# A transformer step on one core: x loaded straight to its place, g applied inside the splits, and a new order at the start

## The chip, the cores and the metric

The kernel runs on one core of one Trainium2 chip. The core has a matrix engine (TensorE, PE in the profile, with PEld for its weight loads), a vector engine (VectorE, DVE), a scalar engine (ScalarE, ACT), a general engine (GpSimd, POOL) and a queue engine (SyncE, SP) that here only issues transfers. Each works through its own queue in order; they wait for each other by semaphores. The metric is the device time of one execution in microseconds, and the profile shows one such execution.

## The reference

One layer of a streaming encoder, for a prompt of 1024 tokens and a sample of 64 tokens, 1088 in all, each of width 1024, in float32:

```
xn = rms_norm(x, g_attn)             # x * rsqrt(mean(x*x)) * g
[rq|rk|rv|rg|sq|sk|sv|ga|gb] = split(xn @ w_in)
a = rms_norm(retention(rope(rq), rope(rk), rv)) * silu(rg) @ w_ret_out
b = window_attention(sq, sk, sv) @ w_swa_out
x += (sigmoid(ga) * a + sigmoid(gb) * b) @ w_mix_out
x += cross_attention(rms_norm(x, g_cross), memory)
x += swiglu(rms_norm(x, g_ffn));  y = rms_norm(x, g_final)
```

The factor rsqrt(mean(x*x)) of a token is a scalar of its column, so the kernel multiplies the raw projections by it afterwards. The vector g runs along the contracted dimension and has to be applied to x (or to the weights) before the product.

## The kernel before

The tokens are the columns: x is held transposed, as 8 tiles of 128 features by 1088 tokens (xT in DRAM). A float32 product is made of three fast ones: each operand is split in a high half, rounded to the format the fast product reads, and a low half, the rest. `split` (L122) does it with a cast on ACT (L123) and a subtraction on DVE (L124). A matrix product is a sum of wh·xh, wh·xl and wl·xh (L205, L206, L208).

The large projections take a pair of weight tiles at a time, in seven half-size products instead of eight (Strassen's scheme, in Winograd's form; `strassen`, L247). It needs x in four quarters, B11, B12 (features 0 to 511, tokens 0 to 543 and 544 to 1087), B21, B22 (features 512 to 1023), and four sums of them: T1 = B12 - B11, T2 = B22 - T1, T3 = B22 - B12, T4 = B21 - T2. Each of these eight operands has 4 tiles of 128x544, split in two halves. The order in which a weight pair uses them is B11, B21, T2, T1, T3, B22, T4 (weights P1, P2, P6, P5, P7, P3, P4; `weight_ops`, L166, forms those with GpSimd, ACT and DVE).

The first pair (the first values, w_v) is computed by `plain` (L225), in eight products from the quarters alone: B11 twice and B12, then B21 twice and B22, then B12 and B22. So it can start while the sums are being formed. `start_phase` (L408), the function that changes, prepares it:

- x comes in 16 pieces of 128x544 into four staging buffers xr, and ACT multiplies each by g into its place xg (L430). A load waits until the multiply has emptied its buffer.
- Behind the pieces of B11 and of B12 a half of the raw weights is loaded (`columns`).
- `operands_early` (L1295) splits B11 and B12, `plain_weights` (L217) the four weight tiles, `operands_late` (L1310) B21 and B22, then forms and splits T1 (through `first_sums`, L1305), T2, T3, T4, each in place of a quarter.

The same `operands_early`, `first_sums` and `operands_late` serve the feed-forward part later, where the tiles come out of a computation and not from DRAM.

After the first pair come, for head 0, the keys (w_k) and queries (w_q) by Strassen's scheme, each rotated on DVE and GpSimd (`rotated`, L581) and stored to DRAM; meanwhile `token_squares` (L443) loads x again and adds up its squares on ACT and DVE into rstd (L452, L454), `token_roots` (L456) turns them into the factors of the tokens (a product with the ones, L463), and `retention` (L691) reads the rotated rows back and transposes them on TensorE (L688).

The program text is not the order on the engines. A planner simulates the kernel and sets each engine's queue, preferring what stands first in the text among what it holds ready. `issue_after(ins)` ties the instructions of a block behind `ins` on its engine; `high_priority` puts a block first.

Of the kernel before, what the change touches and what calls it, by code (L numbers as in the profile page):

```python
# [11 lines left out]
F32 = mybir.dt.float32  # L12
F32R = mybir.dt.float32r
AF = mybir.ActivationFunctionType
ALU = mybir.AluOpType
# [4 lines left out]
P = 128  # L20
D = 1024
KT = D // P
# [17 lines left out]

HALF = T // 2
HC = HALF // 2
OPS = ("B11", "T1", "T2", "B21", "T3", "B22", "T4", "B12")


# [64 lines left out]
class Kernel:  # L110
# [86 lines left out]
    def multiply(self, ps, w, xs, first=True, last=True):  # L197

        mm = self.nc.tensor.matmul
        for k, x in enumerate(xs):  # L200
            ks = slice(k * P, (k + 1) * P)
            start, stop = first and k == 0, last and k == len(xs) - 1
            for c in range(2):
                cs = slice(c * HC, (c + 1) * HC)
                mm(ps[:, c, :HC], w[:, 0, ks], x[:, 0, cs], start=start, stop=False)  # L205
                mm(ps[:, c, :HC], w[:, 0, ks], x[:, 1, cs], start=False, stop=False)  # L206
            for c in range(2):
                self.last_mm = mm(ps[:, c, :HC], w[:, 1, ks], x[:, 0, c * HC:(c + 1) * HC], start=False, stop=stop).ins  # L208
        return ps[:, :, :HC]

# [36 lines left out]
    def strassen(self, w, x, emit, part=False):  # L247


        nc = self.nc  # L250
        u1, u2, u3, u5 = (self.fp.tile([P, 2, HC], F32, tag=t, bufs=1, name=t) for t in ("u1", "u2", "u3", "u5"))
        add = lambda out, a, b: nc.vector.tensor_tensor(out=out, in0=a, in1=b, op=ALU.add)  # L252
# [80 lines left out]
    def run(self):  # L333
        nc, tc, io = self.nc, self.tc, self.io
        with ExitStack() as ctx:
# [25 lines left out]
            self.d_h = [dp.tile([KT, P, T], F32, name=f"d_h{i}") for i in range(2)]  # L361
            self.d_op = dp.tile([len(OPS), FT // 2, P, HALF], F32, name="d_op")
            self.d_rb = dp.tile([16, 64 * 256], F32, name="d_rb")
# [44 lines left out]
    def start_phase(self, ctx):  # L408

        nc, tc, io = self.nc, self.tc, self.io  # L410
        g = self.gains[:, 0, :]
        xg = self.ring_tiles(0, KT // 2, "xg", F32)
        self.xg = [xg[k // 2][:, k % 2, :] for k in range(KT)]
        self.ops, self.slots = {}, {}
        self.new_b12(ctx)
        sp = ctx.enter_context(tc.tile_pool(name="sp", bufs=1, reuse_waits="tile"))
        self.early = [sp.tile([P, 2, HC], F32, name=f"early{i}") for i in range(4)]
        xr = lambda: sp.tile([P, HALF], F32, tag="xr", bufs=4, name="xr")
        raws = [self.wp.tile([P, 1024], F32, tag="raw", bufs=2, name="raw") for i in range(2)]

        def columns(j):
            for i in range(2):
                self.load(raws[i][:, j * 512:(j + 1) * 512].rearrange("p (k m) -> p k m", m=P), io["w_v"][i][:, 4 * j:4 * j + 4])

        def pieces(k0, t):
            hs = slice(t * HALF, (t + 1) * HALF)
            for k in range(k0, k0 + 4):
                x = xr()
                self.load(x, io["xT"][k, :, hs])
                nc.scalar.mul(self.xg[k][:, hs], x, g[:, k:k + 1])  # L430

        for n, (k0, t) in enumerate(((0, 0), (0, 1), (4, 0), (4, 1))):
            pieces(k0, t)
            if n < 2:
                columns(n)
            if n == 1:
                self.operands_early()
        self.load(self.ident, io["c_ident"])
        w = self.plain_weights(raws)
        self.operands_late(self.first_sums)  # L440
        return w

    def token_squares(self):  # L443
# [863 lines left out]
            b11, b12, _, _ = self.quarters(k)  # L1307
            self.put_sum("T1", k, b12, b12, b11)

    def operands_late(self, sums=None):  # L1310
        self.op_tiles(1, ("B21", "B22", "T2", "T3"))
        qs = [self.quarters(k) for k in range(4)]
        for k, (b11, b12, b21, b22) in enumerate(qs):
            self.put_op("B21", k, b21)
        for k, (b11, b12, b21, b22) in enumerate(qs):
            self.put_op("B22", k, b22)
        if sums is not None:
            sums()
        for k, (b11, b12, b21, b22) in enumerate(qs):
            self.put_sum("T2", k, b12, b22, b12)  # L1320
        for k, (b11, b12, b21, b22) in enumerate(qs):
            self.put_sum("T3", k, b11, b12, b11)
        self.op_tiles(0, ("T4",))
        for k, (b11, b12, b21, b22) in enumerate(qs):
            self.put_sum("T4", k, b21, b21, b12)
# [15 lines left out]
    def gate_up(self, pairs):  # L1341
# [12 lines left out]
        for n, fs in enumerate(pairs):  # L1354
# [5 lines left out]
            def save(name, src, n=n):  # L1360
                self.store(self.d_op[OPS.index(name), n], src)

# [67 lines left out]
    def fetch(self, name, group):  # L1430
        n0 = sum(GROUPS[:group]) // 2
        for k in range(GROUPS[group] // 2):
            self.pools = self.pools[1:] + self.pools[:1]
            a = self.pools[0].tile([P, HALF], F32, tag="hl", name="hl")
            self.load(a, self.d_op[OPS.index(name), n0 + k])
            yield a
# [179 lines left out]
```

## Time and profile before

| what | us |
|---|---|
| median of 3 runs | 2260.78 (2258.72 to 2265.74) |
| the profiled execution | 2262.17 |
| its span | 2260.3 |
| mean granted TensorE clock | 0.983 |
| ACT, POOL busy | 896.4, 691.1 |

A row of the timeline gives the start and the duration in microseconds, the engine, the line of the kernel, the operation, its output and inputs with their shapes (partitions x elements) and how many were merged; a bracket gives the idle time of the engine before it and what ended that. A row of waits gives who waited for whom: microseconds in total, times, longest. A group's row gives count, busy time, mean ns of one, then the idle time before them and who ended it. Matmuls overlap, so the distance from start to start tells the pace, not the duration.

### The profile page before, as it was taken

To read this page: it belongs to the slowest core of one execution; us is meant where nothing else is said; L and a number is where in the kernel's file an instruction comes from. 1 tells how busy PE (TensorE), PEld (TensorE's weight loads), DVE (VectorE), ACT (ScalarE), POOL (GpSimd) and SP (SyncE) were. 2 spreads that over 40 slices of the span, in tenths; PEclk is the share of its full clock that TensorE was granted. 3 is DMA by queue.
4 is the path that set the end of the run, shared out by engine and by line. 5 is a ranking of instruction groups with operands and counts; after the bars stand their busy time and mean duration, and the time that the engine had idled before them with its cause. 6 is when DMAs were issued, how large, how long until landed. Compare 5 with 4: busy or idle time off the path is not lost.

```text
span 2260.3 us, 42100 instructions
## 1 busy us (share of the span) xinstructions
PE 2170.2 (96%) x16580; PEld 2117.9 (94%) x16580; DVE 1587.3 (70%) x2673; ACT 896.4 (40%) x1923; POOL 691.1 (31%) x467
## 2 busy tenths in 40 slices
PE   7999999999999989999999999999999999999996
PEld 6999998999999977889999998999999999999996
DVE  8986877766677657885455565776777677778497
ACT  7333333345444355553133343333222222344244
POOL 1441533242244112220000000014556555434462
PEclk9999999999999989999999999999999999999998
DMA  5644445443444466326443112422342332476233
GB/s 191 191 139 133 131 143 143 131 136 113 151 156 148 155 223 203 114 77 214 124 153 118 38 53 69 135 73 88 121 134 94 101 129 80 154 256 195 72 97 108
DMA packets 186408, 298.67 MB, mean 132 GB/s; under 512 B 40514, under 2 KB 111074, under 8 KB 186210
## 3 DMA queue, kind: packets, MB, share of 16 engines
q1 hardware_dynamic: 181602, 287.06, 40.4%
q10 hardware_dynamic: 4608, 8.91, 1.1%
q8 instruction: 131, 2.15, 0.4%
q14 instruction: 67, 0.55, 0.1%
HBM read 204.75 MB, written 91.16 MB: 131 GB/s over the span
## 4 chain that ended last, share of the span: by engine, by line
PE 77%; DVE 12%; DMA 5%; ACT 3%; issue 2%; POOL 1%; SPq 0%; DVEq 0%; ACTq 0%; POOLq 0%
PE pq L205 15%; PE pq L208 15%; PE pq L206 15%; PE pd L149 7%; PE pd L151 7%; PE pd L150 7%; DVE wq L124 2%; DVE B L124 1%; DVE T L124 1%; DMA cs<-c_rope 1%; PE pss L930 1%; DMA hl<-d_op 1%; PE pout L996 1%; PE pp L973 1%; DVE stage L562 1%
## 5 line engine op out<-in xcount | busy, mean ns | idle before, releaser
L123 ACT CAST wq<-raw 128x512 fp32r<-128x512 f32 (+1 forms) x509 | 310.2, 614 | 569.3 <-PE pq L208 289.3
L124 DVE TENSOR_TENSOR wq<-raw,wq 128x512 fp32r<-128x512 f32 (+1 forms) x509 | 450.3, 888 | 120.7 <-ACT wq L123 118.7
L205 PE MATMUL pq<-T,wq 128*128 128x272 f32 x1832 | 503.4, 292 | 4.1 <-DVE T L124 2.7
L206 PE MATMUL pq<-T,wq 128*128 128x272 f32 x1832 | 499.7, 289 | 0.0
L205 PE MATMUL pq<-B,wq 128*128 128x272 f32 x1592 | 439.2, 293 | 11.3 <-ACT wq L123 10.2
L206 PE MATMUL pq<-B,wq 128*128 128x272 f32 x1592 | 437.3, 291 | 9.1 <-DVE B L124 8.9
L208 PE MATMUL pq<-T,wq 128*128 128x272 f32 x1832 | 384.5, 290 | 0.7 <-DVE wq L124 0.6
L183 POOL TENSOR_TENSOR raw<-raw 128x512 f32<-128x512 f32 (+1 forms) x59 | 81.2, 1377 | 890.2 <-DVE wq L124 665.7
L205 PEld LDWEIGHTS pq<-T,wq 128*128 128x128 f32 x1832 | 347.3, 190 | 5.4 <-ACT wq L123 3.6
L206 PEld LDWEIGHTS pq<-T,wq 128*128 128x128 f32 x1832 | 350.6, 191 | 0.3 <-issue 0.3
L208 PE MATMUL pq<-B,wq 128*128 128x272 f32 x1592 | 333.9, 290 | 0.0
L206 PEld LDWEIGHTS pq<-B,wq 128*128 128x128 f32 x1592 | 305.9, 192 | 11.8 <-DVE B L124 11.4
L205 PEld LDWEIGHTS pq<-B,wq 128*128 128x128 f32 x1592 | 303.0, 191 | 12.0 <-ACT wq L123 10.2
L208 PEld LDWEIGHTS pq<-T,wq 128*128 128x128 f32 x1832 | 287.2, 190 | 2.2 <-DVE wq L124 1.5
L208 PEld LDWEIGHTS pq<-B,wq 128*128 128x128 f32 x1592 | 250.1, 190 | 0.5 <-issue 0.3
L252 DVE TENSOR_TENSOR u<-pq,u 128x544 f32<-128x544 f32 x177 | 127.5, 720 | 121.8 <-PE pq L208 121.1
L186 POOL TENSOR_TENSOR raw<-raw 128x512 f32<-128x512 f32 (+1 forms) x59 | 83.2, 1410 | 126.1 <-DVE wq L124 118.4
L562 DVE TENSOR_TENSOR stage<-pq,u 128x544 f32<-128x544 f32 x112 | 80.2, 716 | 28.4 <-PE pq L208 28.3
L958 POOL TENSOR_TENSOR t<-t,den 128x768 f32<-128x768 f32 (+2 forms) x34 | 47.8, 1406 | 145.7 <-DVE den L956 58.4
L184 POOL TENSOR_TENSOR raw<-raw 128x512 f32<-128x512 f32 (+1 forms) x59 | 87.2, 1477 | 3.7
L1450 POOL TENSOR_TENSOR y<-u,y 128x544 f32<-128x544 f32 x38 | 63.3, 1674 | 72.8 <-DVE y L1448 52.9
L189 POOL TENSOR_TENSOR raw<-raw 128x512 f32<-128x512 f32 (+1 forms) x59 | 83.7, 1418 | 4.5
(361 smaller groups left out, 4662.6 us busy)
## 6 DMA issues: line engine op xcount, KB each, us to landing
hl<-d_op SPq DMA_DIRECT2D x85, 272.0 KB, 4.3
d_qkv<-stage SPq DMA_DIRECT2D x44, 272.0 KB, 4.4
d_op<-stage SPq DMA_DIRECT2D x44, 272.0 KB, 2.3
d_op<-ht SPq DMA_DIRECT2D x44, 272.0 KB, 3.5
raw<-w_gate SPq DMA_DIRECT2D x22, 512.0 KB, 3.5
raw<-w_up SPq DMA_DIRECT2D x22, 512.0 KB, 4.3
cs<-c_rope SPq DMA_DIRECT2D x16, 544.0 KB, 4.4
d_gate<-stage ACTq DMA_DIRECT2D x32, 272.0 KB, 2.5
```

The lines of the kernel that those rows point to most:

```text
L123: self.last_cast = self.nc.scalar.copy(hi, src).ins
L124: self.nc.vector.tensor_tensor(out=lo, in0=src, in1=hi.bitcast(F32), op=ALU.subtract)
L149: mm(ps, wh, xh, start=start, stop=False)
L150: mm(ps, wh, xl, start=False, stop=False)
L151: self.last_mm = mm(ps, wl, xh, start=False, stop=stop).ins
L184: tt(out=a21, in0=a21, in1=a22, op=add)
L189: tt(out=a12, in0=a12, in1=a11, op=sub)
L205: mm(ps[:, c, :HC], w[:, 0, ks], x[:, 0, cs], start=start, stop=False)
L206: mm(ps[:, c, :HC], w[:, 0, ks], x[:, 1, cs], start=False, stop=False)
L208: self.last_mm = mm(ps[:, c, :HC], w[:, 1, ks], x[:, 0, c * HC:(c + 1) * HC], start=False, stop=stop).ins
L252: add = lambda out, a, b: nc.vector.tensor_tensor(out=out, in0=a, in1=b, op=ALU.add)
L562: nc.vector.tensor_tensor(out=o, in0=ps, in1=sb, op=ALU.add)
```

## The change

Only `start_phase` changes; `operands_late` loses an argument that nobody else used.

- x is loaded straight into xg, all 16 pieces at once, without staging buffers and without the multiply by g. The weights' halves are loaded in between, by single tile (`columns(i, j)`).
- The split of a quarter applies g itself (`put`): ACT multiplies into the high half, DVE forms x·g minus the high half in one instruction with two operations (scalar_tensor_tensor).
- For the sums, B11 and B12 are multiplied by g in place on ACT, 8 instructions; where T2 is formed from B22 and T4 from B21, the same two-operation instruction applies g.
- The splits come in the order B11, B12, B21, B22, with the four weight splits among those of B11 and B12. All sums are tied behind the last split of B21 on ACT and on DVE. The T's are split in the order T2, T1, T3, T4. T3 is now formed from T2 and B11, the same value.
- Ahead of it all ACT multiplies one column of the ones into a spare tile, which is where its table is loaded, and TensorE makes 20 products of the ones with themselves (WARM = 20) whose result nobody reads.

```diff
+WARM = 20
...
-        xr = lambda: sp.tile([P, HALF], F32, tag="xr", bufs=4, name="xr")
...
+        nc.scalar.mul(self.mtok[:, :1], self.ones[:, :1], 1.0)
+        warm = self.norm_psum("warm")
+        for i in range(WARM):
+            nc.tensor.matmul(warm[:, :P], self.ones, self.ones, start=i == 0, stop=i == WARM - 1)
+
+        def rows(k, t):
             hs = slice(t * HALF, (t + 1) * HALF)
-            for k in range(k0, k0 + 4):
-                x = xr()
-                self.load(x, io["xT"][k, :, hs])
-                nc.scalar.mul(self.xg[k][:, hs], x, g[:, k:k + 1])
-
-        for n, (k0, t) in enumerate(((0, 0), (0, 1), (4, 0), (4, 1))):
-            pieces(k0, t)
-            if n < 2:
-                columns(n)
-            if n == 1:
-                self.operands_early()
+            self.load(self.xg[k][:, hs], io["xT"][k, :, hs])
+
+        def columns(i, j):
+            self.load(raws[i][:, j * 512:(j + 1) * 512].rearrange("p (k m) -> p k m", m=P), io["w_v"][i][:, 4 * j:4 * j + 4])
+
+        rows(0, 0)
+        columns(0, 0)
+        for k in range(1, 4):
+            rows(k, 0)
+        columns(1, 0)
+        for k in range(4):
+            rows(k, 1)
+        for i in range(2):
+            columns(i, 1)
+        for t in range(2):
+            for k in range(4, KT):
+                rows(k, t)
         self.load(self.ident, io["c_ident"])
-        w = self.plain_weights(raws)
-        self.operands_late(self.first_sums)
+
+        self.op_tiles(0, ("B11", "T1"))
+        self.ops["B12"] = [self.b12[:, k] for k in range(4)]
+        self.op_tiles(1, ("B21", "B22", "T2", "T3"))
+        qs = [self.quarters(k) for k in range(4)]
+
+        def put(name, k, src, g):
+            o = self.ops[name][k]
+            hi = nc.scalar.mul(o[:, 0], src, g).ins
+            return hi, nc.vector.scalar_tensor_tensor(o[:, 1], src, g, o[:, 0].bitcast(F32), ALU.mult, ALU.subtract).ins
+
+        w = {}
+
+        def weight(i, j):
+            q = w[i, j] = self.new_op()
+            self.split(raws[i][:, j * 512:(j + 1) * 512], q[:, 0, :512], q[:, 1, :512])
+
+        for n, name in enumerate(("B11", "B12", "B21", "B22")):
+            for k in range(4):
+                put_by = put(name, k, qs[k][n], g[:, k + 4 * (n // 2):k + 4 * (n // 2) + 1])
+                if n == 2:
+                    behind = put_by
+                if k == 0 and n < 2:
+                    weight(0, n)
+                if k == 2 and n < 2:
+                    weight(1, n)
+        with tc.issue_after(behind[0]), tc.issue_after(behind[1]):
+            for k in range(4):
+                b11, b12 = qs[k][:2]
+                for b in (b11, b12):
+                    nc.scalar.mul(b, b, g[:, k:k + 1])
+                nc.vector.tensor_tensor(out=b12, in0=b12, in1=b11, op=ALU.subtract)
+        for k, (b11, b12, b21, b22) in enumerate(qs):
+            nc.vector.scalar_tensor_tensor(b22, b22, g[:, k + 4:k + 5], b12, ALU.mult, ALU.subtract)
+            self.put_op("T2", k, b22)
+        for k, (b11, b12, b21, b22) in enumerate(qs):
+            self.put_op("T1", k, b12)
+        for k, (b11, b12, b21, b22) in enumerate(qs):
+            self.put_sum("T3", k, b11, b22, b11)
+        self.op_tiles(0, ("T4",))
+        for k, (b11, b12, b21, b22) in enumerate(qs):
+            nc.vector.scalar_tensor_tensor(b21, b21, g[:, k + 4:k + 5], b22, ALU.mult, ALU.subtract)
+            self.put_op("T4", k, b21)
         return w
```

More of the change, by code (lines that the diff above doesn't have):

```diff
@@ L417, in start_phase @@
         self.early = [sp.tile([P, 2, HC], F32, name=f"early{i}") for i in range(4)]
-        xr = lambda: sp.tile([P, HALF], F32, tag="xr", bufs=4, name="xr")
         raws = [self.wp.tile([P, 1024], F32, tag="raw", bufs=2, name="raw") for i in range(2)]
[L421 to L425, printed above, removed]
-            hs = slice(t * HALF, (t + 1) * HALF)
-            for k in range(k0, k0 + 4):
-                x = xr()
-                self.load(x, io["xT"][k, :, hs])
-                nc.scalar.mul(self.xg[k][:, hs], x, g[:, k:k + 1])
@@ L1308, in first_sums, with operands_late @@
             self.put_sum("T1", k, b12, b12, b11)
-    def operands_late(self, sums=None):
+    def operands_late(self):
         self.op_tiles(1, ("B21", "B22", "T2", "T3"))
@@ L1316, in operands_late @@
             self.put_op("B22", k, b22)
-        if sums is not None:
-            sums()
         for k, (b11, b12, b21, b22) in enumerate(qs):
```

## The prediction

> **What bounds the kernel now.** I first read the summary's busy shares: TensorE is busy 96% of the span, so the question is where the other 4% lies and which part of it the change can reach. All the edited code sits in the first 50 us. The table by stage (columns: busy time and instructions of PE, its weight loads, DVE, ACT and POOL, then granted clock, DMA share, GB/s) shows these stretches:
>
> ```profile
> PE 2170.2 (96%) x16580; PEld 2117.9 (94%) x16580; DVE 1587.3 (70%) x2673; ACT 896.4 (40%) x1923; POOL 691.1 (31%) x467
> ...
> 0.00:10.00 10.00, 0.00 (x0) 0.00 (x0) 1.99 (x5) 5.96 (x9) 0.20 (x4) 1.00 0.77 244
> 10.00:20.00 10.00, 9.82 (x67) 9.82 (x68) 9.07 (x15) 10.00 (x19) 0.00 (x0) 1.00 0.92 299
> 20.00:30.00 10.00, 6.32 (x47) 5.65 (x45) 10.00 (x13) 10.00 (x18) 3.32 (x2) 1.00 0.39 124
> 30.00:40.00 10.00, 7.98 (x59) 7.54 (x60) 10.00 (x17) 4.87 (x9) 0.00 (x0) 1.00 0.15 57
> 40.00:50.00 10.00, 9.90 (x79) 9.69 (x78) 9.28 (x13) 7.21 (x13) 3.38 (x2) 1.00 0.57 192
> 50.00:60.00 10.00, 10.00 (x82) 10.00 (x82) 8.47 (x14) 5.22 (x9) 1.18 (x1) 1.00 0.88 297
> 80.00:90.00 10.00, 8.06 (x65) 7.96 (x65) 9.44 (x12) 2.48 (x5) 9.21 (x6) 0.92 0.49 156
> 90.00:100.00 10.00, 8.45 (x51) 8.16 (x50) 8.75 (x19) 3.08 (x6) 4.65 (x3) 0.74 0.39 116
> 100.00:120.00 20.00, 16.75 (x120) 16.02 (x119) 16.24 (x38) 5.14 (x10) 7.26 (x5) 0.91 0.47 138
> ```
>
> Two things are to be seen. TensorE does nothing for 10 us, then loses 3.7 + 2.0 us between 20 and 40, is full from 40 to 80, and loses 1.9 + 1.6 + 3.3 us between 80 and 120. DVE, by contrast, has hardly a gap from 10 to 100. So early on there are two clocks: TensorE's, with over 15 us to win, and DVE's, with little. Which one sets the end is the whole question. The waits of TensorE in the first 110 us, and the timeline rows around the gaps (start, duration, engine, line, operation, tiles, and in brackets the idle time before), name the causes:
>
> ```profile
> PE pq L205 <- ACT wq L123: 10.2, 1, 10.2
> PE pq L206 <- DVE B L124: 5.5, 3, 2.6
> ...
> 1.17 2.78 DMA xr<-xT
> ...
> 4.02 1.28 ACT L430 ACT_TABLE_LOAD   x1 [4.02 <-DMA xr<-xT]
> 5.32 1.39 ACT L430 ACTIVATE xg<-xr,gains 128x544 f32<-128x544 f32 x2
> 6.61 0.63 ACT L123 CAST B<-xg 128x544 fp32r<-128x544 f32 x1
> 7.27 0.72 DVE L124 TENSOR_TENSOR B<-xg,B 128x544 fp32r<-128x544 f32 x1 [6.26 <-ACT B L123]
> ...
> 10.58 0.43 PE L206 MATMUL pq<-B,wq 128*128 128x272 f32 x1
> 10.80 0.43 PE L205 MATMUL pq<-B,wq 128*128 128x272 f32 x1
> ...
> 13.70 0.29 PE L205 MATMUL pq<-B,wq 128*128 128x272 f32 x1
> 13.82 0.29 PE L206 MATMUL pq<-B,wq 128*128 128x272 f32 x1
> ...
> 42.80 0.29 PE L205 MATMUL pq<-B,wq 128*128 128x272 f32 x1
> ```
>
> The first product waits 10.2 us for ACT, which is loading a table, multiplying x by g and casting. Its first matmuls start 0.22 us apart, from 13.70 on 0.125 us: the slow clock lasts some 3 us. Three times B21 and B22 come late from DVE (5.5 us in all), because the sums for T1 to T4 stand between them. At 42.80 the first eight-product block (24 us of matmuls) is over and the next weight pair begins.
>
> **The change part by part.** All durations are from this one execution: 2262.17 us, of which the span is 2260.3. The median of the three runs shown is 2260.78, 1.4 us less; I subtract from the median.
>
> *Early table load.* The 1.28 us at 4.02 move before the data, to the time when ACT only waits. ACT's first product of x then starts at 4.0 instead of 5.32: 1.3 us, hidden behind the first transfer. [...]
>
> *g inside the split.* Before, an operand costs ACT a multiply and a cast, and DVE a subtraction. After, ACT multiplies straight into the high half, DVE forms the low half with a scalar_tensor_tensor that multiplies and subtracts. So 16 casts go, and 8 extra multiplies (B11 and B12 for the sums) come on top of the 16. The work per tile in the list by form, and the nearest rows of both DVE operations at one shape:
>
> ```profile
> L430 ACT ACTIVATE xg<-xr,gains 128x544 f32<-128x544 f32 x16 | 11.7, 746 | 0.0
> ...
> L123 ACT CAST B<-xg 128x544 fp32r<-128x544 f32 x24 | 14.9, 641 | 0.6 <-DVE xg L1256 0.3
> ...
> L269 DVE SCALAR_TENSOR_TENSOR xc<-ld,gains,xc x24: 546/618/620, 1145.4 to 1238.1; 128x384 fp32r<-128x384 f32 x16, 128x320 fp32r<-128x320 f32 x8
> ...
> L124 DVE TENSOR_TENSOR mix<-ld,mix x24: 491/558/561, 1055.1 to 1141.5; 128x384 fp32r<-128x384 f32 x16, 128x320 fp32r<-128x320 f32 x8
> ```
>
> ACT: 8 multiplies more (8 x 0.75) less 16 casts (16 x 0.64): 4 us less, on an engine that is full from 10 to 30. DVE: the medians are 618 against 558 ns, 0.06 us more each. The count on DVE stays 52 (16 low halves, 4 weight splits, 16 sums, 16 low halves of T), 24 of them of the dearer kind (16 halves, 4 sums for T2, 4 for T4): 24 x 0.06 = 1.4 us lost. Bounds: 0 if the extra time overlaps the instruction before, 2.4 at 0.1 each.
>
> *x straight to its place.* The same 16 loads of x and 4 of w_v, so nothing on the DMA side but the order; no load waits for one of four staging buffers any more. Their 5.5 MB at the 299 GB/s of the second stretch take 18.4 us, so the last piece lands near 21. B21's last piece has 4.4 MB ahead of it and itself, landing near 17, its halves ready near 18.5; TensorE wants it at about 19. SP's queue gets freer, which helps the w_k loads and the identity behind.
>
> *Products of ones.* 20 matmuls of 128x128 in float32, two instructions each. The nearest rows are a fast-clock and a slow-clock group of that form:
>
> ```profile
> 223.38 1.16 PE L473 MATMUL pb<-ident,rtok 128*128 128x128 f32 x8
> 224.30 0.37 PE L206 MATMUL pq<-T,wq 128*128 128x272 f32 x1
> ...
> 2251.46 1.65 PE L1539 MATMUL pb<-ident,rs_f 128*128 128x128 f32 x6 [1.29 <-DVE rs_f L294]
> ```
>
> Fast: 0.92 us for 4 products, 0.23 each. Slow: (1.65 - 0.42) / 5 x 2 = 0.49 each. The ones are there at 1.0 us; with 3.3 us of slow clock, as from 10.18 on, 7 products are slow and 13 fast: 3.3 + 3.0, so they end at 7.5. The first product of w_v could otherwise begin at 3.95 (x landed) + 0.65 + 0.52 (weight cast) with its load a little later, near 5.7. So the ones cost 1.8 us of start and buy 13 matmul steps of 0.1 us, 1.3 us. Bounds: ending at 6 (fast early) to 10.9 (20 x 0.49, slow throughout).
>
> *Order of use.* With B21 and B22 split ahead of all sums, DVE has 20 operations (20 x 0.64 + 16 x 0.06 = 13.8 us) from 4.65 on, with some 2 us of waiting for data, as now (rows below: 10.87 us busy in the 12.73 from 7.27 on): all B's are ready at 20.4, against 25.6 when TensorE reaches B22. The 5.5 us of stalls go. The new wait (the sums issue behind B21's last split on ACT and on DVE) holds 8 multiplies and 4 subtractions, and behind them the T's. T2 comes at 20.4 + 4 x 0.64 + 8 x 0.67 + three weight halves at 0.6 = 30.1; the third product of w_k wants it at 7.5 + 24.1 + 6.0 = 37.6. Cover: 7 us.
>
> **The sum.** TensorE's clock: start 10.18 to 7.5 is 2.7, slow clock 1.3, stalls 5.5: 9.5 us by the time the next weight pair begins. DVE's clock: it starts 2.6 us earlier (7.27 to 4.65), loses 1.4 to the dearer operation, keeps its early waits, wins the 0.7 of idle between 40 and 50, the 1.1 for which the sum of squares waits for ACT (row below; the squares can start when the first block ends), and some 0.5 between 80 and 90: 3.5 us. What decides is the first point at which TensorE must wait for DVE. The rows for it, from the table by stage, DVE's waits from 50 to 60, and TensorE's timeline:
>
> ```profile
> 7.27:20.00 12.73, 9.82 (x67) 9.82 (x68) 10.87 (x17) 12.73 (x23) 0.00 (x0) 1.00 0.93 303
> ...
> 48.90:97.20 48.30, 44.72 (x337) 44.11 (x335) 46.21 (x61) 20.85 (x36) 24.13 (x14) 0.93 0.62 193
> ...
> DVE rstd L454 <- ACT xsq L452: 1.1, 1, 1.1
> ...
> 85.34 2.05 PE L463 MATMUL pt<-ones,rstd 128*128 128x2 f32 x18
> 89.33 1.12 PE L688 MATMUL pk<-ident,ks 128*128 128x128 f32 x4 [1.94 <-DMA ks<-d_qkv]
> 90.70 0.43 PE L205 MATMUL pq<-B,wq 128*128 128x272 f32 x1
> ```
>
> Between 48.9 and 97.2 DVE is busy 46.2 of 48.3 us. The transposes of the first retention block wait for rows which DVE has rotated and which went out and back through DRAM; the sums of squares (L454) are DVE's too. An earlier TensorE only waits longer there. I expect 3.5 to 4 us of the 9.5 to reach the end: 2260.8 - 3.8 = 2257. After 120 us TensorE is nearly full and carries the shift on. Own range of this case: 2254 to 2259, from the bounds on the dearer operation and about 1 us either way for DVE's waits for data.
>
> **Rivals.** (a) *TensorE's clock carries*: what DVE still owes at 85 can be put off, or the products of the next pair are set ahead of the transposes. For it: TensorE did run a w_k product at 90.70 between two transposes. Against it: the row of 46.2 in 48.3. It gives 2260.8 - 9.5 = 2251.
>
> (b) *A wait replaces the removed one*: the first w_k halves stand on DVE behind all sums, which are now always ready. DVE ends its 52 operations at 4.65 + 1.9 + 52 x 0.64 + 1.4 = 41.2, so the next pair begins near 41 instead of 42.8, and 0 to 2 us are left: 2260.
>
> (c) *Slower*: the order on each engine is planned for the whole program, so a start that moves 10 us is a new order everywhere behind. Its place would be the retention's output transposes, which already wait:
>
> ```profile
> L812 PE MATMUL pb<-ident,ret_o 128*128 128x128 f32 x64 | 13.2, 296 | 11.7 <-ACT ret_o L808 11.7
> ```
>
> Waits of over 2 us are followed by the slow clock (0.226 us steps from 90.70 on, clock 0.74), worth 0.1 us x 26 matmuls. If these 11.7 us double, and two of the waits bring the slow clock, 11.7 + 5 - 3.8 = 13 us are lost: 2274. From 3.8 us of new waits on it is a loss. I take a half as typical, 2268. For it speaks only that the waits exist.
>
> (d) *The ones overrun*: should the clock stay slow through all 20, they end at 10.9, TensorE starts 0.7 later than now, and its clock still wins 1.3 + 5.5 - 0.7 = 6.1, over DVE's 3.5; the end would lose at most 1 us: 2258. [...]
>
> **How the numbers follow.** Chances: forecast 0.45, (a) 0.25, (b) 0.12, (c) 0.13, (d) 0.05. A measurement of this kernel can tell about 0.3%, 6.8 us, from no change; so 2254 and 2267.6 are the limits. Faster: nearly all of (a), 0.23, and the lower edge of the forecast, 0.11. Slower: (c), less its mild part, and some unnamed, 0.13. The rest, 0.53, is no measurable change. The range takes in (a) with 4 us below it, since the gaps at 109 to 115 might close too, and a mild (c): 2247 to 2265.
>
> **What would show it.** First product of w_v between 7 and 8.5 at steps of 0.125 us; no wait for B from DVE above 1 us; w_k's first product at 32 to 34 (right for TensorE's clock) or near 41, (b). Then the gap ahead of the first retention transposes should be longer than now, by some 5 us, with the transposes 3 to 5 us earlier: that is the forecast. If the gap doesn't grow, it is (a). Scalar_tensor_tensor at 128x544 should last 0.78 us, not 0.72. I am wrong if DVE's queue between 45 and 100 holds fewer operations than now, or if new waits of over 2 us stand behind 120 us.

## The result, and the profile after

The changed kernel takes 2267.16 us against 2260.85 us (medians of 20 runs each), a ratio of 1.0023 with an interval of 1.0013 to 1.0033 (worked out from the fast single runs, so it is not the ratio of the two medians). Two later comparisons, on chips 12 and 7, gave 1.0001 (0.9991 to 1.0012) and 1.0014 (1.0004 to 1.0024). So the change does not make the kernel faster: by the three ratios it costs 5.2, 0.2 and 3.2 us, and whether it costs anything at all stays open. Forecast were 2257 us, in a range from 2247 to 2265.

The table by stage of the changed kernel (columns as before):

```profile
0.00:10.00 10.00, 8.95 (x52) 8.95 (x53) 4.08 (x8) 5.95 (x9) 0.20 (x4) 1.00 0.77 246
10.00:20.00 10.00, 10.00 (x82) 10.00 (x81) 8.88 (x13) 9.79 (x16) 0.00 (x0) 1.00 1.04 369
20.00:30.00 10.00, 9.89 (x79) 9.67 (x79) 8.89 (x14) 10.00 (x18) 0.00 (x0) 1.00 0.30 110
30.00:40.00 10.00, 9.18 (x74) 8.96 (x72) 10.00 (x14) 5.73 (x10) 4.60 (x2) 1.00 0.58 193
40.00:50.00 10.00, 2.41 (x9) 2.09 (x10) 10.00 (x14) 6.87 (x13) 3.32 (x2) 0.56 0.33 117
50.00:60.00 10.00, 10.00 (x63) 10.00 (x64) 8.70 (x14) 3.65 (x7) 1.74 (x2) 0.75 0.65 214
```

The start did what it was meant to do. TensorE is full from 10 to 39, where it had lost 6 us. But between 40 and 50 it works 2.4 us in 10, and 63 instructions in the stretch after it instead of 82 show the slow clock (granted 0.50 of full speed from 41.29 to 54.94). The waits of TensorE in the first 120 us:

```profile
PE pq L206 <- ACT wq L124: 6.1, 1, 6.1
PE pk L735 <- DMA ks<-d_qkv: 2.9, 1, 2.9
PE pss L150 <- ACT qs L124: 2.8, 1, 2.8
PE pq L209 <- DVE wq L125: 2.3, 1, 2.3
```

The 10.2 us for the first weight and the 5.5 us for B21 and B22 are gone; 6.1 and 2.3 us have come instead, for weights. Which weights, the timelines of the four engines tell (changed kernel):

```profile
1.05 7.63 PE L423 MATMUL warm<-ones 128*128 128x128 f32 x40 [1.05 <-DVE rtok L350]
8.44 0.37 PE L206 MATMUL pq<-B,wq 128*128 128x272 f32 x1
...
45.26 0.59 PE L206 MATMUL pq<-T,wq 128*128 128x272 f32 x1 [6.08 <-ACT wq L124]
45.65 0.43 PE L207 MATMUL pq<-T,wq 128*128 128x272 f32 x1
...
49.77 0.82 PE L209 MATMUL pq<-T,wq 128*128 128x272 f32 x2 [2.33 <-DVE wq L125]
...
5.27 0.79 DVE L454 SCALAR_TENSOR_TENSOR B<-xg,gains,B 128x544 fp32r<-128x544 f32 x1 [4.25 <-ACT B L453]
...
19.36 0.73 DVE L476 TENSOR_TENSOR xg<-xg 128x544 f32<-128x544 f32 x1 [0.55 <-ACT xg L475]
...
31.38 1.28 DVE L125 TENSOR_TENSOR wq<-raw,wq 128x512 fp32r<-128x512 f32 x2
...
33.85 1.82 DVE L478 SCALAR_TENSOR_TENSOR xg<-xg,gains,xg 128x544 f32<-128x544 f32 x1
35.59 1.81 DVE L125 TENSOR_TENSOR T<-xg,T 128x544 fp32r<-128x544 f32 x1
...
41.20 0.68 DVE L125 TENSOR_TENSOR wq<-raw,wq 128x512 fp32r<-128x512 f32 x1
...
44.15 3.69 DVE L125 TENSOR_TENSOR T<-xg,T 128x544 fp32r<-128x544 f32 x4
...
49.04 0.68 DVE L125 TENSOR_TENSOR wq<-raw,wq 128x512 fp32r<-128x512 f32 x1
...
35.70 0.65 ACT L124 CAST T<-xg 128x544 fp32r<-128x544 f32 x1
...
44.60 2.16 ACT L124 CAST wq<-raw 128x512 fp32r<-128x512 f32 x4
...
32.14 2.94 POOL L184 TENSOR_TENSOR raw<-raw 128x512 f32<-128x512 f32 x1 [31.70 <-DVE wq L125]
...
41.95 1.69 POOL L187 TENSOR_TENSOR raw<-raw 128x512 f32<-128x512 f32 x1 [5.14 <-DVE wq L125]
```

The third product of the keys (the first with T) needs the key weight P6, and P6 stands at the end of a chain: P1 is split, its low half made on DVE (31.38); GpSimd then forms the next difference (32.14); P7 is split, its low half on DVE (41.20); only then may GpSimd overwrite it (41.95) and ACT cast P6 (44.60). P6's own low half comes on DVE at 49.04. Each link on DVE stands in the queue among the sums for the T's.

The product's other operand, T2, is late too. L478 forms it; the last of its four sums starts at 33.85, and ACT casts that tile at 35.70. The profile leaves out the numbers of the T's, but the order of the program's instructions tells which is which: the low half of this tile is the first of the four at 44.15, whole near 45.9, behind splits of T1 and sums and splits of T3 and T4. TensorE, which ended the second product at 39, would have wanted it near 41.3. So the third product lacked both operands, and the weight came last.

Rows of the weights before the change, and of the third product there:

```profile
20.43 0.68 DVE L124 TENSOR_TENSOR wq<-raw,wq 128x512 fp32r<-128x512 f32 x1
...
44.14 0.68 DVE L124 TENSOR_TENSOR wq<-raw,wq 128x512 fp32r<-128x512 f32 x1
...
48.86 1.88 DVE L124 TENSOR_TENSOR wq<-raw,wq 128x512 fp32r<-128x512 f32 x3
...
48.83 0.29 PE L205 MATMUL pq<-T,wq 128*128 128x272 f32 x1
...
49.59 0.52 PE L208 MATMUL pq<-T,wq 128*128 128x272 f32 x2
```

TensorE began the third product at 48.83, and the first instruction to read P6's low half (L208), made from 48.86 on, started at 49.59, a quarter of a microsecond behind the usual pace. That wait was hidden almost exactly, so the view of waits did not show it. After the change the low half comes at 49.04: TensorE arrives 10 us earlier, and DVE is no earlier at all.

To see what reaches the end I set the start of each matmul in one trace against the same matmul in the profile before, and took the median shift by stretches (us; the left column is the time before). The kernels on which the argument rests stand in it:

```
at       after  P6 tied  before, no   after, no    P6 tied, no
                (e8)     squares (e9) squares(e10) squares (e11)
36-42    -9.7   -9.7     +2.6         -9.7         -9.9
48.8-52   0.0  -10.1     +2.2         -0.6        -10.3
64-80    +2.0   -1.9     +2.2         +1.4         -2.6
86-101   +2.9   -5.9     +1.8         -4.3         -8.5
150-200  +2.5   -1.8     +1.8         -3.9         -5.2
450-600  +6.8   -0.2     -0.7         +0.2         -9.1
2200-    +5.3   -0.4     -5.4         -0.8         -7.9
```

In the changed kernel 9.7 us are won at 40 us, nothing is left at 50, and 2.0 are lost at 64, where the slow clock after the wait (0.50, to 54.94) has had its turn. The two last rows of a single profile also carry the spread between executions: the kernel before without the squares ends 5.4 us ahead there, while its ratio below is 1.0000.

### The profile page after: what moved, and what is told of

Its sections match the earlier page's. It is cut to its first block, busy times and chain, and to the rows that moved or that the text cites. A ratio compares the mean times of both kernels' runs of the same rounds, so it can differ in the third digit from the quotient of the medians.

```text
span 2266.5 us, 42175 instructions
## 1 busy us (share of the span) xinstructions
PE 2180.8 (96%) x16620; PEld 2128.6 (94%) x16620; DVE 1587.3 (70%) x2673; ACT 892.7 (39%) x1916; POOL 691.1 (30%) x467
## 4 chain that ended last, share of the span: by engine, by line
PE 75%; DVE 12%; DMA 7%; ACT 3%; issue 2%; POOL 1%; SPq 0%; DVEq 0%; ACTq 0%; POOLq 0%
PE pq L206 15%; PE pq L209 15%; PE pq L207 14%; PE pd L150 7%; PE pd L152 7%; PE pd L151 7%; DVE wq L125 2%; DMA cs<-c_rope 2%; DMA hl<-d_op 1%; PE pss L977 1%; DVE T L125 1%; PE pout L1043 1%; PE pp L1020 1%; DVE stage L644 1%; DVE stage L609 1%
## 5 line engine op out<-in xcount | busy, mean ns | idle before, releaser
L206 PEld LDWEIGHTS pq<-T,wq 128*128 128x128 f32 x1832 | 348.9, 190 | 11.6 <-ACT wq L124 10.2
```

## The experiments

Ratios are against the kernel before, run on the same chip. **First four: which term matters.**

*The sums behind P7.* T1's splits, T3 and T4 move behind the text of the key weights and are tied to P7's low half on DVE:

```diff
             first = pair("w_k", 0)
+            with tc.issue_after(self.los["P7"]):
+                last_sums()
```

> Edit to the changed kernel: the splits of T1 and the forming and splitting of T3 and T4 stand behind the low half of the key weight P7 on DVE. Theory (the chain of the key weights P1, GpSimd, P7, GpSimd, P6 stands on DVE among the sums, and so TensorE loses at the third key product what it won before): the waits of 6.1 and 2.3 us at that product fall below 3 us together, the slow clock from 41 to 55 us goes, the third product begins near 40 us instead of 45.3, and the time falls by 5 to 9 us against the changed kernel, to 2258 to 2262. Rival (DVE's whole work up to the first retention block sets the pace, wherever its parts stand): the waits move to the retention transposes near 90 us, which start within 1.5 us of where they do now, and the time stays within 2 us of 2267.

1.0003 (0.9993 to 1.0012). The third product then begins at full clock near 39 (matmuls 0.13 us apart from 38.77 on), but the low half of its weight still stands behind the sums; the waits of TensorE, and DVE's row of T2's low halves:

```profile
PE pq L211 <- DVE wq L126: 5.2, 1, 5.2
...
29.09 2.63 DVE L126 TENSOR_TENSOR T<-xg,T 128x544 fp32r<-128x544 f32 x4
```

T2 is now whole at 31.7 and P6's high half came earlier too, its low half only at 44.79. So with x in time P6's low half alone holds TensorE for 5.2 us, where waits below 3 were expected. The time itself lies where the theory put it, 2260.80; but its fall of 5 to 9 us is counted from the 2267 of the first comparison, which did not come back (below), and so says little.

*Without the ones.*

```diff
-        warm = self.norm_psum("warm")
-        for i in range(WARM):
-            nc.tensor.matmul(warm[:, :P], self.ones, self.ones, ...)
```

> Edit to the changed kernel: the 20 products of the ones are left out, the early table load stays. Theory (the weight chain sets the third key product): the first product of w_v begins near 6 us instead of 8.4, at the slow clock for some 3 us, so the first block ends 1 us earlier or the same, the third key product still begins at 45 us, and the time stays within 2 us of 2267. Rival (TensorE's own clock counts): the time changes by what the first block's end changes, and if the ones were what disturbs the slow clock later, it falls by more than 3 us.

1.0002 (0.9992 to 1.0011). The timeline of TensorE shows the first product at 6.09 instead of 8.44, at the slow clock (0.23 us from start to start, against 0.13 from 8.65 on in the changed kernel):

```profile
6.09 0.59 PE L206 MATMUL pq<-B,wq 128*128 128x272 f32 x1 [6.09 <-ACT wq L124]
6.48 0.43 PE L207 MATMUL pq<-B,wq 128*128 128x272 f32 x1
```

At 36 us it is 7.9 us ahead of before, 1.8 less than with the ones, and at 50 us neither is ahead: the ones win 1.8 us in a place where it is worth nothing. The third key product began at 46.39, about as the theory has it; the time, 2261.84, did not stay within 2 us of 2267.

*g in place.* ACT multiplies x where it lies, then plain casts and subtractions:

```diff
-            hi = nc.scalar.mul(o[:, 0], src, g).ins
-            return hi, nc.vector.scalar_tensor_tensor(o[:, 1], src, g, ...).ins
+            nc.scalar.mul(src, src, g)
+            hi = nc.scalar.copy(o[:, 0], src).ins
+            return hi, nc.vector.tensor_tensor(out=o[:, 1], in0=src, in1=..., op=ALU.subtract).ins
```

> Edit to the changed kernel: g is multiplied into x in place on ACT (16 multiplies) and the quarters and sums are split and formed by plain casts and subtractions, as before; order, loads, table and ones stay. Theory (DVE's clock at the low half of P6 decides, and the two-operation instruction costs it 0.07 us 24 times): that low half comes 1 to 2 us earlier than 49.0, unless ACT, with 4 us more work, falls behind; the time falls by 0 to 3 us. Rival (ACT's extra work delays the B quarters): TensorE waits for B22 or T2 for over 1 us and the time rises by 1 to 4 us.

0.9997 (0.9987 to 1.0008): not to be told from before, nor surely from after. P6's low half was not earlier (50.91), so the expected 1 to 2 us didn't show there. ACT held TensorE for 2.0 us with its copies out of the first block and for 1.7 us in two splits of B, much as the rival has it, but the time did not rise.

*Ones and table added to the kernel before.*

```diff
+        nc.scalar.mul(self.mtok[:, :1], self.ones[:, :1], 1.0)
+        warm = self.norm_psum("warm")
+        for i in range(WARM): ...
```

> Edit to the kernel before: only the early table load and the 20 products of the ones are added. Theory: the first product begins 0.5 to 1.3 us earlier at full clock, but the third key product still begins when its weight is there, at 48.8; the time stays within 1.5 us of the kernel before, 2260.9. Rival (TensorE's clock carries): 2 to 2.6 us faster, 2258.5.

1.0016 (1.0005 to 1.0027): slower in this one comparison, which neither expected. At 48.8 us the shift is 0.9 us ahead, as the theory has it; the loss comes between 125 and 300, and by which step is not shown.

**Second four: the ones, and P6 properly freed.** Leaving out the ones seemed to gain 5 us on the median (2261.84 against 2267.16, in another session), though every other instruction kept its order on its engine. So the kernel itself ran again beside two variants of the ones (`WARM = 1`; ten products in each of two tiles).

> The changed kernel as it is, on the same chip as the three that follow, so that they can be compared with it directly. Its cost of 0.23% should come back: 2265 to 2268.

> Edit to the changed kernel: one product of the ones instead of 20; its PSUM tile stays. Leaving all 20 out made it 5 us faster although every engine's order stayed the same. Theory a (the time that the products take, or the clock that they bring, is what costs): as fast as without them, 2261 to 2262.5. Theory b (the one PSUM tile more shifts which of the two buffers the later tiles of that pool get): as slow as the changed kernel, 2265 to 2268.

> Edit to the changed kernel: the 20 products of the ones go to two PSUM tiles in turn, ten each, so that the later tiles of the two-buffer pool fall on the same buffers as without the ones. Theory a (the products or their clock cost): as slow as the changed kernel, 2265 to 2268. Theory b (the shifted buffers cost): as fast as without the ones, 2261 to 2262.5.

The unchanged text of the changed kernel gave 1.0001 (0.9991 to 1.0012), one product 0.9994 (0.9984 to 1.0003), two tiles 1.0001 (0.9990 to 1.0012). The intervals overlap and the repeat itself missed its expectation, so neither theory of the ones stands; whether they cost 0.1% stays open. With the repeat at 2261.69, every gain of the first four that is counted from 2267 falls away; what stands are the ratios to the kernel before on the same chip.

*The sums behind P6*: as behind P7, with `self.los["P6"]`.

> Edit to the changed kernel: as in the run with the sums behind P7, but the splits of T1 and all of T3 and T4 stand behind the low half of P6. There the low half of P6 still came at 44.8 us and TensorE waited 5.2 us for it. Theory (the place of P7 and P6 on DVE sets the third key product): P6 is whole before 39.5 us, the third key product runs through at full clock from 40 us on, with waits below 1.5 us. Whether that reaches the end: if TensorE's clock carries from there, the time is 2254 to 2257; if DVE's work up to the first retention block takes it back, it is 2259 to 2263, and the products behind it or the retention transposes wait instead.

0.9996 (0.9987 to 1.0004). The third product begins at 39.05 at full clock (1.00 from 40 to 50) and the shift at 48.8 is still -10.1. T2 is whole at 32.0 and P6 at 38.4. So the splits and sums of the other T's, in DVE's queue ahead of T2's last half, P7 and P6, are what cost the 8.4 us. But nothing reaches the end. Rows of this run, from DVE's timeline (T2 and P6), TensorE's waits, the table by stage, and TensorE's timeline:

```profile
29.37 2.63 DVE L126 TENSOR_TENSOR T<-xg,T 128x544 fp32r<-128x544 f32 x4
...
37.12 1.24 DVE L126 TENSOR_TENSOR wq<-raw,wq 128x512 fp32r<-128x512 f32 x1 [2.05 <-ACT wq L125]
...
PE pq L208 <- ACT T L125: 3.8, 1, 3.8
PE pq L211 <- DVE wq L126: 3.8, 3, 1.6
...
48.90:97.20 48.30, 41.44 (x310) 40.54 (x310) 48.30 (x59) 19.07 (x32) 24.76 (x14) 0.96 0.51 160
...
83.72 0.95 PE L514 MATMUL pt<-ones,rstd 128*128 128x2 f32 x8
88.69 0.66 PE L741 MATMUL pk<-ident,ks 128*128 128x128 f32 x4 [0.82 <-DMA ks<-d_qkv]
97.64 1.75 PE L514 MATMUL pt<-ones,rstd 128*128 128x2 f32 x10 [1.37 <-DVE rstd L505]
106.47 0.60 PE L741 MATMUL pk<-ident,vf 128*128 128x128 f32 x4
```

DVE is busy for 48.30 of 48.30 us. What the sums no longer delay, they delay next: T4 and the last weights (3.8 and 3.8 us), then the sum of squares, whose product with the ones goes on to its second part only at 97.64, where it all stood at 85.34 before.

**Third four: take work from DVE.** If DVE is the second limit, then sparing it alone must give nothing, freeing P6 alone nothing, and both together the win. 14 additions of squares are 9 us of DVE:

```diff
                 nc.scalar.activation(x if k else acc, x, AF.Square)
-                if k:
-                    nc.vector.tensor_tensor(out=acc, in0=acc, in1=x, op=ALU.add)
```

These three leave out seven eighths of the sum of squares, so they compute something else than the layer.

> Edit to the kernel before: the 14 additions on DVE that sum up the squares of x are left out (only one of eight squares per token counts, so the factors of the tokens are others). They are 9 us of DVE's work, 11.6 with what GpSimd stretches, between 49 and 85 us. Theory (DVE's work up to the first retention block sets where TensorE is at 100 us): DVE has 9 us to spare, but TensorE itself reaches the transposes at 87.4, so they begin 1 to 3 us earlier than 89.3, and the time falls by 1 to 4 us, to 2257 to 2260. Rival (the round trip of the rotated rows through DRAM sets it, not DVE): less than 1 us.

> The same 14 additions left out of the changed kernel. Theory: some of them stand on DVE ahead of the low half of P6, so this comes 1 to 2 us earlier than 49.0; TensorE still waits for the weight chain, reaches the transposes no earlier than the kernel before, and the time is within 2 us of the kernel before with the same left out. Rival (TensorE's clock counts once DVE is free): 4 us or more faster than that one.

> The same 14 additions left out of the changed kernel with the sums behind P6. Theory: both clocks are free now, so the win at the start must reach the end: the first retention transposes come 4 to 8 us earlier than in the kernel before with the same left out, and the time is 3 to 8 us below that one, 2250 to 2256. Rival (the win is lost in the round trip through DRAM whatever DVE does): within 2 us of it.

Before without them 1.0000 (0.9989 to 1.0011); after without them 0.9986 (0.9976 to 0.9996); with the sums behind P6, without them, 0.9976 (0.9965 to 0.9988), 2255.11 us. The last is 5.0 us below the kernel before with the same cut (2260.15), and its first retention transposes come 4.4 us earlier than there (85.18 against 89.56), both as expected; they stand together, instead of at 89.33 and 96.76 in the kernel before (TensorE's timeline):

```profile
85.18 0.66 PE L739 MATMUL pk<-ident,ks 128*128 128x128 f32 x4 [2.26 <-DMA ks<-d_qkv]
85.67 0.60 PE L739 MATMUL pk<-ident,vf 128*128 128x128 f32 x4
```

And here most of TensorE's shift stays, -8.5 at 86 us and -7.9 at the end, as the table of shifts shows. The changed kernel without the additions lies between, at 2259.10 us: P6's low half came only 0.6 us earlier (48.44), but TensorE reached the transposes at 87.81, which that expectation did not have. In the kernel before the same cut empties DVE (35.64 us busy in the stretch) and the time doesn't move:

```profile
48.90:97.20 48.30, 44.22 (x353) 44.00 (x352) 35.64 (x46) 21.21 (x36) 21.42 (x14) 0.97 0.64 212
```

The expectation of 1 to 4 us there was wrong. In this profile TensorE reaches the product of squares at 87.58 and goes on to the transposes without a wait: there it is TensorE that limits. It is 2.2 us later than in the profile before, and has been since 36 us: between 30 and 40 us its granted clock was 0.66 here and 1.00 there. So the two limits lie within a few us of each other, but how far apart this cut doesn't tell. Nor do these three separate DVE's 9 us from the chain of the squares itself, which the cut shortens as well.

*The additions on GpSimd* (`nc.gpsimd` for `nc.vector`, nothing left out, sums behind P6):

> The changed kernel with the sums behind P6, and the 14 additions of squares moved from DVE to GpSimd (nothing left out). Theory: GpSimd needs 1.3 to 1.8 us for each, 14 x 1.6 = 22 us, in a stretch where it is busy 24 of 48 us, and DVE is stretched whenever GpSimd works; half of the 9 us are given back to the stretching, 1 to 4 us are won: 2257 to 2260. Rival (GpSimd becomes the bound of the square sums): the product with the ones behind them waits, and the time rises by 2 to 6 us.

1.0027 (1.0014 to 1.0039): a rise of some 6 us, as the rival has it, but not by the rival's way, a wait of the product with the ones. The group of GpSimd from 30 to 120 us, TensorE's waits, and rows of DVE and ACT:

```profile
L505 POOL TENSOR_TENSOR rstd<-rstd,xsq 128x544 f32<-128x544 f32 x14 | 25.9, 1852 | 12.0 <-ACT xsq L503 11.4
...
PE pq L208 <- ACT T L125: 10.5, 1, 10.5
...
44.46 6.12 DVE L490 SCALAR_TENSOR_TENSOR xg<-xg,gains 128x544 f32<-128x544 f32 x4
50.51 3.55 DVE L126 TENSOR_TENSOR wq<-raw,wq 128x512 fp32r<-128x512 f32 x2
...
56.50 1.19 ACT L125 CAST T<-xg 128x544 fp32r<-128x544 f32 x2 [5.03 <-DVE T L126]
```

TensorE waits 10.5 us for T4's cast (56.50), and the cast waits for DVE. Six of the additions run on GpSimd from 44.44 to 55.25, and beside them DVE's four sums for T4 take 6.1 us, where those of the run with the sums behind P7 take 2.9, and two weight halves 3.6 us instead of 1.3.

**Last two.** The third comparison, and P6 freed with g in place and without the ones.

> The changed kernel as it is, a third comparison. If the loss belongs to the kernel: a ratio of 1.0015 to 1.003. If it belonged to the first session: 0.9995 to 1.0012.

> Edit to the changed kernel: sums behind P6, g multiplied into x in place on ACT with plain splits, and no products of the ones. Theory (DVE's work to the first retention block takes back what TensorE wins): DVE is spared 1.4 us of dearer instructions, so the time falls by 1 to 2 us against the run with the sums behind P6 alone, a ratio of 0.9988 to 0.9996. Rival (three separate small wins that add up at the end): a ratio below 0.9985.

1.0014 (1.0004 to 1.0024), between the two expectations; and 1.0002 (0.9992 to 1.0012): no small wins add up, and the 1 to 2 us by the theory aren't seen either. No complete kernel tried is surely faster than the one before.

## Why the prediction was wrong, point by point

**TensorE's clock: right in its sum, not term by term.** 9.5 us were forecast by the next weight pair, 9.7 came. The start gave 1.7 us (8.44 against 10.18) and not 2.7: the slow clock of the ones lasted to 7.16 us, some 6 us and not 3.3; with all 20 at the slow clock, rival (d)'s case, they were to end at 10.9, and they ended at 8.68. The rest, with the waits for B21 and B22 gone, gave 8.0 us and not 6.8; what the 1.2 us more are is not shown. That the two errors cancel is luck.

**DVE's clock: the right limit, a wrong sum.** The forecast had DVE 3.5 us earlier; at P6's low half it was 0.2 us later (49.04 against 48.86). Of the terms, the start was 2.0 us earlier, not 2.6 (5.27 against 7.27), and the dearer instruction cost what was said, 0.78 against 0.72 us. The idle time did not shrink: from its first split to P6's low half DVE stands idle 3.1 us, 2.6 before. The four differences for T1 each wait about half a microsecond for the multiplies by g that the change puts ahead of them on ACT (row 19.36: 0.55), some 2.2 us between 17 and 22, which take back what the earlier waits gave.

**The step that failed** is "Cover: 7 us", where T2 was to be ready at 30.1 and the third product to want it at 37.6. Behind the quarters the sum put only T1's four differences, T2's sums and low halves and three weight halves in DVE's queue. In the run B22 was whole at 28.8, not 20.4: its first split waits on ACT behind the eight multiplies by g (16.7 to 21.9), and its last low half on DVE behind other sums. The splits of T1 and sums and splits of T3 and T4, ready by then too, stood among those of T2. So T2 was whole near 45.9, about 16 us later than forecast. P6, which hangs on P7 by way of GpSimd, each link in the same queue, was whole at 49.7. TensorE, there at 39, waited 6.1 and 2.3 us, and the slow clock behind the waits (0.50 to 54.94) took the rest. Rival (b) named this mechanism but set it at the first key weight and at 0 to 2 us left; it happened at the third, P6, and left nothing. The tied runs show it: with the other T's behind P7, T2 is whole at 31.7 and P6's low half alone costs 5.2 us; with them behind P6 the wait is gone.

**That an earlier TensorE only waits longer for DVE** fits the runs: the squares left out of the kernel before gave nothing (1.0000), P6 freed gave nothing that can be told (0.9996), both together 0.24%. The 3.5 to 4 us that were to reach the end all the same did not. The changed kernel without the squares, with P6 as late as ever, stands between at 0.9986, so the picture of two limits is not a sharp one.

**The later loss.** The shift grows from 2.5 to 6.8 us between 300 and 450 us in the first profile. The order on every engine there is the same as before, and the two repeats lie lower. The retention's waits for ret_o, rival (c)'s place, are 10.5 us there against 8.2 in 300 to 460. That the times at which the clock changes (below) make the difference is a guess of mine, not shown. That the first comparison's 2267 lies beside (c)'s 2268 is luck: over the whole profile those waits went from 11.7 to 14.7 us and did not double, and they were 15.5 us in the repeat whose ratio is 1.0001. What (c) says of waits over 2 us holds for ten of the twelve behind the first product in the profile before; those of 2.60 us, which ends at 25.24, and of 2.67, which ends at 1044.97, brought no slow clock. Nor is 2 us a limit: the slow clock in (c)'s example, 0.50 from 88.44 to 95.27, came with a wait of 1.94 us, which ends at 89.33.

## What to carry to other kernels

A wait that is almost exactly hidden has no row: before moving an engine forward, list for each of its next few inputs, weights as well as data, when they are ready, and follow each back through all the engines that form it. When an engine beside the bound one is full for the whole stretch, count what the change does to that engine's last needed instruction, not to its first, with everything in its queue that will be ready by then, whether or not it is needed. And to find two limits that lie close together, take each away alone and then both; a single cut that gives nothing does not show that the thing cut is free.

## What the runs showed of the hardware

In the records of both profiles TensorE's granted clock is either 1.00 or 0.50, and it changes on a grid. In the profile before, slow stretches begin at 88.44, 115.75 and 255.70 us and last 6.83, 3.41 and 3.41; in the one after they begin at 41.29, 92.49 and 116.38 and last 13.65, 6.83 and 3.41. The differences of all these times are whole multiples of 3.413 us within a profile, and the remainder is another in each (3.11 and 0.33). In the changed kernel the full clock first came at 7.16 us, on the grid of the others. The row of the ones lasts 7.63 us there and 6.64 in the kernel before with the ones, though they began at 1.05 in both. What makes the clock change is not shown.

Some instructions of DVE and GpSimd that overlap last longer. In the changed kernel a DVE subtraction of 128x544 took 1.81 us instead of 0.72 (35.59) while GpSimd worked from 35.16 to 36.82, and a GpSimd difference of 128x512 took 2.94 us (32.14) beside a full DVE, where the same line's mean is 1.42. It is not so "whenever GpSimd works", as the expectation of the additions on GpSimd has it: in the changed kernel's profile 296 of DVE's two-input instructions of 128x544 (additions, subtractions, products) overlap one of GpSimd, and 35 of them take over 1.5 us; of the 507 that meet none, none takes over 0.73.
